# A hybrid mLSTM, attention and expert layer: shorter VectorE chains in the head norm, the gates' maximum and the convolution, with the bias copies later and the value pool opened early

## The chip, the core and the metric

One core of a Trainium2 chip runs the whole layer for 1024 tokens in one launch. The metric is the device time of that launch in microseconds, the median of several runs. The engines are TensorE (PE, with its weight loads as PEld), VectorE (DVE), ScalarE (ACT), GpSimd (POOL) and SyncE (SP), which here only issues DMAs. Each engine works through its own list of instructions in order; engines wait for one another by semaphores.

## The reference

x has 1024 tokens of 1024 channels. What is computed, cut to what matters:

```python
h = rms_norm(x, norm1_g)
u, vm, z, ipre, fpre, qa, ka, va = split(h @ w_in)          # 512 each, the gates 4 each
c = silu(causal_short_conv(u, conv_w, conv_b))              # 4 taps
hm = mlstm_chunkwise(qm, km, vm, ipre + ig_b, fpre + fg_b)  # 4 heads x 128, chunks of 128
ym = sigmoid(z) * (rms_norm(hm, mh_norm_g) + skip_m * c)
ya = combine(dilated_branch(qh, kh, vh, rel_bias, w, d) for 3 patterns)   # 8 heads x 64
x = x + concatenate([ym, ya]) @ w_out
h2 = rms_norm(x, norm2_g)
x = x + peer(h2)   # 8 heads, 128x128 product keys, top 16: 128 experts of 16384 a token
```

In `mlstm_chunkwise` each head's output is h = num / max(|den|, exp(-m)), and the norm over its 128 channels follows. The stabiliser m is a running maximum, carried from chunk to chunk as max(b_last + m, m_loc). For a token, `peer` takes gelu(h2 . u_e) times a gate for each of its experts e and sums the rows v_e.

## The kernel before

Tokens lie in eight tiles of 128, in three groups: tiles 0 and 1 (group 0), 2 to 5 (group 1), 6 and 7 (group 2). For each group come a norm and transpose of x, the products with w_in (values vm and gate z in `project_values`, gates in `project_gates`, u with the convolution in `project_conv`, attention's q, k, v in `project_attention`), attention woven with the mLSTM's chunks, w_out (`acco`), the products with w_query (`accq`) and the top-k picks. A product is done in three passes of rounded halves (high by high, low by high, high by low): ScalarE rounds a weight block (`wh`, L168), VectorE takes the remainder (`wl`, L170), and SP loads the block (`wr`, L166).

The experts are done in two ways. For group 1 all 16384 experts are computed densely on TensorE: `pu` (h2 by u) and `pv` (by v), after the gates have been spread over the experts by products `pg` and a copy to memory (`gate_d`, `gg`). For groups 0 and 2 the 128 experts of each token are gathered by indirect DMAs that GpSimd issues (L801), 128 of 512 KB for each tile and direction, in the order U0 U1 V0 V1 U6 V6 U7 V7. VectorE consumes a U gather in one instruction of 128x1024 (L813, `gt<-gt,h2s`, with a small read of the sum behind it), a V gather of tiles 6 and 7 likewise (L858), and TensorE consumes those of V0 and V1 (`pov`, L844). Gathers begin once group 0's picks are known and run beside everything that follows.

The order of each engine's instructions isn't the program's text: a scheduler of the framework keeps a modelled timeline and puts out each engine's list by it, so an edit at one place can move instructions at others. Pools set further limits: a pool that takes over another's memory waits for its last reader.

What the change and the prediction touch:

- `skew` (L132 to L134): eight copies of the position bias to memory, one per attention head, 128x1152 floats; attention's `bt` loads (L491) read them.
- `project_conv` (L255 to L278): per channel block of 128, ScalarE copies the product to `uh` behind a halo of three columns (L266 to L268), VectorE makes the first tap with the bias into `cy` (L270) and adds three more (L273), then ScalarE's sigmoid and VectorE's product follow (L275, L276).
- `project_values` (L280) with its pool "sa" and the evictions `ev`.
- `gates` (L361 to L395): softplus on ScalarE, a cumulative sum `bc` by scans (L368), `gi` (L369), then per tile a running maximum `mr` (L372) whose start is the carried maximum `mst`, and the next `mst` from its last column (L373); four rows are transposed to columns by TensorE (`pc`, L387).
- the end of each mLSTM head (L455 to L472): `sm` holds five columns for two tiles; |den| and its maximum (L457, L458), reciprocal, its square, the scaled sum of squares (L459 to L461), `rstd` (L159 on VectorE, the power at L161 on GpSimd), the product (L463), the normed head `hn` (L465), its transpose `pth` (L468).

Of the kernel before, what the change touches and what calls it, by code (L numbers as in the profile page):

```python
# [20 lines left out]
P = 128  # L21
# [22 lines left out]
def hybrid_layer(ctx, tc, x, g1, w_in, w_if, conv_w, conv_b, wq, wk, if_b, mh_g, skip, qn_g, kn_g,  # L44
# [86 lines left out]
    skew_d = {}  # L131
    for h in range(AH):  # L132
        skew_d[h] = dram.tile([P, RL], F32, name=f"skew{h}")
        nc.sync.dma_start(skew_d[h], rel_d[h:h + 1].to_broadcast([P, RL]))  # L134

# [121 lines left out]
    def project_conv(g, th, tl):  # L257
# [3 lines left out]
        with pool("su") as st:  # L261
            for blk in range(2):
                accs = by_channel(stream(w_in, blk, th, tl, n, True, "u"), n)
                for h, a in enumerate(accs, 2 * blk):
                    uh = st.tile([P, 3 + W], F32, name="uh", bufs=2)
                    nc.vector.tensor_copy(uh[:, 0:3], halo[:, h])  # L266
                    nc.scalar.copy(uh[:, 3:], a)
                    nc.vector.tensor_copy(halo[:, h], uh[:, W:W + 3])  # L268
                    y = st.tile([P, W], F32, name="cy", bufs=2)
                    nc.vector.tensor_scalar(y, uh[:, 0:W], cw_s[:, h, 0:1], cb_s[:, h:h + 1],  # L270
                                            op0=ALU.mult, op1=ALU.add)
                    for j in range(1, 4):
                        nc.vector.scalar_tensor_tensor(y, uh[:, j:j + W], cw_s[:, h, j:j + 1], y,  # L273
                                                       op0=ALU.mult, op1=ALU.add)
                    nc.scalar.activation(uh[:, 0:W], y, AF.Sigmoid)  # L275
                    nc.vector.tensor_tensor(y, y, uh[:, 0:W], op=ALU.mult)  # L276
                    c_d[g, h] = dram.tile([P, W], F32, name=f"c{g}{h}")
                    nc.sync.dma_start(c_d[g, h], y)  # L278

    def project_values(g, th, tl):  # L280

        n = GROUPS[g][1]
        W = n * P
        with pool("sa") as st:
            token_blocks(g, st, 2, vm_d, "vm", th, tl)
# [69 lines left out]
    def gates(g, cl, ml, gi, gf):  # L355
# [10 lines left out]
        for c in range(n):  # L366
            f = gf[:, c * P:(c + 1) * P]
            nc.vector.tensor_tensor_scan(bc[:, c], f, f, 0.0, op0=ALU.add, op1=ALU.bypass)  # L368
        nc.vector.tensor_tensor(gi, gi, bc, op=ALU.subtract)  # L369
        for c in range(n):  # L370
            t = tile0 + c
            nc.vector.tensor_tensor_scan(mr[:, c], gi[:, c], gi[:, c], mst[:, t:t + 1], op0=ALU.max, op1=ALU.max)  # L372
            nc.vector.tensor_tensor(mst[:, t + 1:t + 2], mr[:, c, P - 1:P], bc[:, c, P - 1:P], op=ALU.add)  # L373
        pc = pst.tile([P, 4, n, MH], F32, name="pc", tag="tp")
# [23 lines left out]
    def mlstm(g, half, h, ml, cols, mix):  # L398
# [59 lines left out]
        nc.vector.tensor_tensor(sm[:, 1], sm[:, 1], ecol[:, 1, :, h], op=ALU.max)  # L458
        nc.vector.reciprocal(sm[:, 2], sm[:, 1])  # L459
        nc.vector.tensor_tensor(sm[:, 3], sm[:, 2], sm[:, 2], op=ALU.mult)  # L460
        nc.vector.tensor_tensor(sm[:, 3], sm[:, 3], sm[:, 0], op=ALU.mult)  # L461
        r = rstd(sm[:, 3], P, HT, ml, "rm")
        nc.vector.tensor_tensor(sm[:, 4], r, sm[:, 2], op=ALU.mult)  # L463
        hn = ml.tile([P, HT, P], F32, name="hn", tag="w2m", bufs=5 if g == 0 else 6)
# [414 lines left out]
    project_conv(0, *hx)  # L879
    project_values(0, *hx)  # L880
    project_attention(0, *hx)
    mx = Scope("mx", "right")
    mix = zq.tiles.tile([P, KD, GROUPS[0][1] * P], F32, name="mix0", tag="z")
    drain(weave(attention(0, mx.tiles, mix), mlstm_half(0, 0, mx.tiles, cols, mix), 4))
    mx.close()
    hx = channels_in(1, hs.tiles)
    pt_ = Scope("pt0", "right")
    drain(queries(0, ql.tiles, "left", cl.tiles, mix))
    for t in range(2):
        pick(pt_.tiles, 0, t, cl.tiles)  # L890
    pt_.close()
    project_values(1, *hx)
    cols = project_gates(1, cm.tiles, *hx)
# [134 lines left out]
```

## Time and profile before

| | us |
|---|---|
| median of 3 runs | 3063.17 |
| lowest and highest | 3061.2, 3078.7 |
| the profiled execution | 3072.45 |
| its span in the trace | 3070.7 |
| busy: TensorE, VectorE | 2752.9, 2355.9 |
| busy: GpSimd, ScalarE | 1423.7, 1231.2 |

The span runs from the first to the last instruction of the trace; the profiled execution's own time is 1.75 us longer. The mean granted clock of TensorE over the span is 0.932 of full speed. A row of waits names the waiting engine, the line, what it waited for, and the sum, count and longest of such waits. Durations of matmuls overlap, so a mean duration is longer than the distance from one to the next.

### The profile page before, as it was taken

The numbers are of one execution on the slowest core, as the hardware profiler recorded it, in microseconds if no ns is written. First come the engines' busy times: TensorE is split into PE (matmuls) and PEld (weight loads), VectorE is DVE, ScalarE is ACT, GpSimd is POOL, SyncE is SP. The second block draws the span as 40 slices with busy tenths as digits, with TensorE's granted clock in tenths as the row PEclk, the third lists the DMA queues.
The fourth block names the chain that finished last, engine by engine and source line by source line (L and its number), as shares of the span: only waits on it lengthen the run. The fifth ranks groups of instructions, "written<-read, shape, count | busy, mean of one in ns | idle before, by whom it ended". The sixth has DMA issues, their size and how long they took to land.

```text
span 3070.7 us, 43024 instructions
## 1 busy us (share of the span) xinstructions
PE 2752.9 (90%) x14382; PEld 2174.1 (71%) x14382; DVE 2355.9 (77%) x5611; ACT 1231.2 (40%) x2271; POOL 1423.7 (46%) x1139
## 2 busy tenths in 40 slices
PE   6978757798849999889888999999999999999999
PEld 5868557576637565567655887887888787888787
DVE  4559887679874697758874888888998888898853
ACT  4643323354413323589985222332332232333222
POOL 0100567447673444544553455455555555555510
PEclk9979878587869998899998999999999999999999
DMA  6644789789898898798889999999999999999952
GB/s 196 182 149 125 263 296 338 267 317 312 311 334 294 288 322 291 235 330 297 316 298 310 321 335 319 317 335 327 335 329 356 335 315 336 338 337 317 334 181 76
DMA packets 370900, 891.52 MB, mean 290 GB/s; under 512 B 34120, under 2 KB 135496, under 8 KB 366581
## 3 DMA queue, kind: packets, MB, share of 16 engines
q0 software_dynamic: 147456, 536.94, 49.4%
q1 hardware_dynamic: 209076, 307.78, 30.6%
q10 hardware_dynamic: 14144, 44.05, 3.8%
q8 instruction: 113, 1.85, 0.2%
q14 instruction: 111, 0.90, 0.1%
HBM read 831.97 MB, written 61.38 MB: 291 GB/s over the span
## 4 chain that ended last, share of the span: by engine, by line
PE 31%; DMA 7%; issue 7%; DVE 6%; POOL 4%; ACT 2%; POOLq 0%; DVEq 0%; SPq 0%; ACTq 0%
DMA gg<-gate_d 5%; PE pu L154 5%; PE pu L153 5%; PE pu L155 5%; PE pv L154 5%; PE pv L155 5%; PE pv L153 5%; POOL gt L801 4%; DVE hot L722 1%; PE pg L737 1%; DMA gt<-in_expert_u_dram,idx 1%; ACT gs L738 1%; DMA vr<-in_expert_v_dram 1%; PE pov L844 1%; DVE gt L813 1%
## 5 line engine op out<-in xcount | busy, mean ns | idle before, releaser
L801 POOL DMA_INDIRECT gt<-in_expert_u_dram,idx x512 | 679.0, 1326 | 629.3 <-DVE gt L813 370.8
L813 DVE SCALAR_TENSOR_TENSOR gt<-gt,h2s 128x1024 f32<-128x1024 f32 x512 | 617.5, 1219 | 79.5 <-DMA gt<-in_expert_u_dram,idx 78.8
L801 POOL DMA_INDIRECT gt<-in_expert_v_dram,idx x256 | 342.2, 1337 | 281.5 <-DVE acc L858 237.3
L154 PE MATMUL pv<-vlo,dah 128*128 128x512 f32 x1024 | 402.8, 394 | 14.2 <-DVE vlo L790 14.2
L801 POOL DMA_INDIRECT gt<-in_expert_v_dram,idxt x256 | 270.1, 1055 | 310.6 <-PE pov L844 247.8
L153 PE MATMUL pu<-h2th,uhi 128*128 128x512 f32 x1024 | 406.4, 397 | 1.2 <-ACT da L763 1.2
L155 PE MATMUL pu<-h2th,ulo 128*128 128x512 f32 x1024 | 406.3, 397 | 0.7 <-DVE ulo L758 0.7
L154 PE MATMUL pu<-h2tl,uhi 128*128 128x512 f32 x1024 | 406.5, 397 | 0.0
L155 PE MATMUL pv<-vhi,dal 128*128 128x512 f32 x1024 | 401.0, 392 | 0.0
L788 ACT CAST vhi<-vr 128x512 fp32r<-128x512 f32 x256 | 158.2, 621 | 459.2 <-PE pv L155 411.8
L858 DVE SCALAR_TENSOR_TENSOR acc<-gt,act,acc 128x1024 f32<-128x1024 f32 x256 | 327.8, 1281 | 16.3 <-DMA gt<-in_expert_v_dram,idx 14.0
L153 PE MATMUL pv<-vhi,dah 128*128 128x512 f32 x1024 | 317.6, 394 | 13.9 <-ACT dah L149 11.9
L168 ACT CAST wh<-wr 128x512 fp32r<-128x512 f32 x291 | 178.6, 621 | 292.2 <-DMA wr<-in_w_in_dram 54.8
L170 DVE TENSOR_TENSOR wl<-wr,wh 128x512 fp32r<-128x512 f32 x291 | 199.4, 691 | 79.0 <-ACT wh L168 71.3
L154 PEld LDWEIGHTS pv<-vlo,dah 128*128 128x128 f32 x1024 | 193.3, 189 | 61.2 <-DVE vlo L790 19.1
L153 PEld LDWEIGHTS pv<-vhi,dah 128*128 128x128 f32 x1024 | 193.3, 189 | 59.3 <-ACT dah L149 12.3
L790 DVE TENSOR_TENSOR vlo<-vr,vhi 128x512 fp32r<-128x512 f32 x256 | 175.2, 686 | 76.5 <-ACT vhi L788 74.4
L756 ACT CAST uhi<-ur 128x1024 fp32r<-128x1024 f32 x128 | 134.5, 1051 | 235.7 <-PE pu L154 228.1
L153 PEld LDWEIGHTS pu<-h2th,uhi 128*128 128x128 f32 x1024 | 192.7, 188 | 49.8 <-issue 1.7
L154 PEld LDWEIGHTS pu<-h2tl,uhi 128*128 128x128 f32 x1024 | 192.8, 188 | 47.6 <-issue 2.5
L155 PEld LDWEIGHTS pu<-h2th,ulo 128*128 128x128 f32 x1024 | 192.8, 188 | 46.8 <-DVE ulo L758 1.3
L155 PEld LDWEIGHTS pv<-vhi,dal 128*128 128x128 f32 x1024 | 193.6, 189 | 42.1
(280 smaller groups left out, 5727.2 us busy)
## 6 DMA issues: line engine op xcount, KB each, us to landing
ur<-in_expert_ut_dram SPq DMA_DIRECT2D x128, 512.0 KB
vr<-in_expert_v_dram SPq DMA_DIRECT2D x256, 256.0 KB
wr<-in_w_in_dram SPq DMA_DIRECT2D x144, 256.0 KB
gate_d<-gs ACTq DMA_DIRECT2D x32, 1024.0 KB
gg<-gate_d SPq DMA_DIRECT2D x16, 2048.0 KB
wr<-in_w_query_dram SPq DMA_DIRECT2D x96, 256.0 KB
wr<-in_w_out_dram SPq DMA_DIRECT2D x48, 256.0 KB
gt<-in_expert_u_dram,idx POOLq DMA_INDIRECT x512
```

Source lines behind the costliest of these rows:

```text
L153: nc.tensor.matmul(ps, lh, rh, start=first, stop=False)
L154: nc.tensor.matmul(ps, lh, rl, start=False, stop=False)
L155: nc.tensor.matmul(ps, ll, rh, start=False, stop=last)
L168: nc.scalar.copy(wh, wr)
L170: nc.vector.tensor_tensor(wl, wr, wh.bitcast(F32), op=ALU.subtract)
L722: nc.vector.tensor_tensor(o, ids[:, side, None, c0:c0 + half].to_broadcast(full), key128, op=ALU.is_equal)
L756: nc.scalar.copy(uh, ur)
L788: nc.scalar.copy(vh, vr)
L790: nc.vector.tensor_tensor(vl, vr, vh.bitcast(F32), op=ALU.subtract)
L801: nc.gpsimd.indirect_dma_start(out=gt, out_offset=None, in_=table, in_offset=bass.IndirectOffsetOnAxis(ap=idx[:, j:j + 1], axis=0))
L813: nc.vector.scalar_tensor_tensor(gt, gt, 1.0, h2, op0=ALU.mult, op1=ALU.mult, accum_out=pr[:, j:j + 1])
L858: nc.vector.scalar_tensor_tensor(acc, gt, COEF[t][:, j:j + 1], acc, op0=ALU.mult, op1=ALU.add)
```

## The change

Four edits. The end of each head loses the reciprocal and two more VectorE operations: with d = max(|den|, exp(-m)), the factor on num is (sum of squares / 128 + EPS d d) to the power -0.5, formed in two combined instructions and one power on GpSimd. The carried maximum of the gates is formed by one reduction over each tile and one scan over the tiles, so that each tile's running maximum no longer hands over to the next. The convolution's first tap, with its bias, is an Identity activation on ScalarE that reads the scale and the bias as columns. The bias copies stand in the text after group 0's products, and the pool of group 1's values is opened before the pool of group 0's picks, in its own place.

```diff
@@ -129,9 +129,11 @@
         nc.sync.dma_start(rel_d, rv)
 
     skew_d = {}
-    for h in range(AH):
-        skew_d[h] = dram.tile([P, RL], F32, name=f"skew{h}")
-        nc.sync.dma_start(skew_d[h], rel_d[h:h + 1].to_broadcast([P, RL]))
+
+    def skew(heads):
+        for h in heads:
+            skew_d[h] = dram.tile([P, RL], F32, name=f"skew{h}")
+            nc.sync.dma_start(skew_d[h], rel_d[h:h + 1].to_broadcast([P, RL]))
 
 
     halo = consts.tile([P, MH, 3], F32, name="halo")
@@ -267,8 +269,7 @@
                     nc.scalar.copy(uh[:, 3:], a)
                     nc.vector.tensor_copy(halo[:, h], uh[:, W:W + 3])
                     y = st.tile([P, W], F32, name="cy", bufs=2)
-                    nc.vector.tensor_scalar(y, uh[:, 0:W], cw_s[:, h, 0:1], cb_s[:, h:h + 1],
-                                            op0=ALU.mult, op1=ALU.add)
+                    nc.scalar.activation(y, uh[:, 0:W], AF.Identity, scale=cw_s[:, h, 0:1], bias=cb_s[:, h:h + 1])
                     for j in range(1, 4):
                         nc.vector.scalar_tensor_tensor(y, uh[:, j:j + W], cw_s[:, h, j:j + 1], y,
                                                        op0=ALU.mult, op1=ALU.add)
@@ -277,11 +278,11 @@
                     c_d[g, h] = dram.tile([P, W], F32, name=f"c{g}{h}")
                     nc.sync.dma_start(c_d[g, h], y)
 
-    def project_values(g, th, tl):
+    def project_values(g, th, tl, st=None):
 
         n = GROUPS[g][1]
         W = n * P
-        with pool("sa") as st:
+        with (nullcontext(st) if st else pool("sa")) as st:
             token_blocks(g, st, 2, vm_d, "vm", th, tl)
             for blk in range(2):
                 accs = by_channel(stream(w_in, 4 + blk, th, tl, n, True, "z"), n)
@@ -367,10 +368,14 @@
             f = gf[:, c * P:(c + 1) * P]
             nc.vector.tensor_tensor_scan(bc[:, c], f, f, 0.0, op0=ALU.add, op1=ALU.bypass)
         nc.vector.tensor_tensor(gi, gi, bc, op=ALU.subtract)
+
+        top = ml.tile([MH, n], F32, name="top")
+        nc.vector.tensor_reduce(top, gi, AX.X, ALU.max)
+        nc.vector.tensor_tensor_scan(mst[:, tile0 + 1:tile0 + n + 1], top, bc[:, :, P - 1],
+                                     mst[:, tile0:tile0 + 1], op0=ALU.max, op1=ALU.add)
         for c in range(n):
             t = tile0 + c
             nc.vector.tensor_tensor_scan(mr[:, c], gi[:, c], gi[:, c], mst[:, t:t + 1], op0=ALU.max, op1=ALU.max)
-            nc.vector.tensor_tensor(mst[:, t + 1:t + 2], mr[:, c, P - 1:P], bc[:, c, P - 1:P], op=ALU.add)
         pc = pst.tile([P, 4, n, MH], F32, name="pc", tag="tp")
         for q in range(4):
             row = gi
@@ -456,11 +461,10 @@
         dn = num[:, :, P]
         nc.vector.scalar_tensor_tensor(sm[:, 1], dn, -1.0, dn, op0=ALU.mult, op1=ALU.max)
         nc.vector.tensor_tensor(sm[:, 1], sm[:, 1], ecol[:, 1, :, h], op=ALU.max)
-        nc.vector.reciprocal(sm[:, 2], sm[:, 1])
-        nc.vector.tensor_tensor(sm[:, 3], sm[:, 2], sm[:, 2], op=ALU.mult)
-        nc.vector.tensor_tensor(sm[:, 3], sm[:, 3], sm[:, 0], op=ALU.mult)
-        r = rstd(sm[:, 3], P, HT, ml, "rm")
-        nc.vector.tensor_tensor(sm[:, 4], r, sm[:, 2], op=ALU.mult)
+
+        nc.vector.scalar_tensor_tensor(sm[:, 2], sm[:, 1], EPS, sm[:, 1], op0=ALU.mult, op1=ALU.mult)
+        nc.vector.scalar_tensor_tensor(sm[:, 3], sm[:, 0], 1.0 / P, sm[:, 2], op0=ALU.mult, op1=ALU.add)
+        nc.gpsimd.tensor_tensor(sm[:, 4], sm[:, 3], mhalf.to_broadcast([P, HT]), op=ALU.pow)
         hn = ml.tile([P, HT, P], F32, name="hn", tag="w2m", bufs=5 if g == 0 else 6)
         nc.vector.tensor_tensor(hn, num[:, :, 0:P], sm[:, 4, :, None].to_broadcast([P, HT, P]), op=ALU.mult)
         pt = pml.tile([P, HW], F32, name="pth", tag="ml")
@@ -878,18 +882,21 @@
     cols = project_gates(0, cm.tiles, *hx)
     project_conv(0, *hx)
     project_values(0, *hx)
+    skew(range(AH))
     project_attention(0, *hx)
     mx = Scope("mx", "right")
     mix = zq.tiles.tile([P, KD, GROUPS[0][1] * P], F32, name="mix0", tag="z")
     drain(weave(attention(0, mx.tiles, mix), mlstm_half(0, 0, mx.tiles, cols, mix), 4))
     mx.close()
     hx = channels_in(1, hs.tiles)
+    sv = Scope("sv", "right")
     pt_ = Scope("pt0", "right")
     drain(queries(0, ql.tiles, "left", cl.tiles, mix))
     for t in range(2):
         pick(pt_.tiles, 0, t, cl.tiles)
     pt_.close()
-    project_values(1, *hx)
+    project_values(1, *hx, sv.tiles)
+    sv.close()
     cols = project_gates(1, cm.tiles, *hx)
     project_conv(1, *hx)
     project_attention(1, *hx)
```

What becomes of the lists: in SP's list one weight block stands between the first skew copy and the other seven, where all eight stood ahead of it; the blocks after it and the `bt` loads keep their places. In VectorE's list 235 gather consumers stand ahead of the last `hn` of group 1, 246 before. In TensorE's list 39 rows of `acco` move from behind the last `pth` of group 1 to ahead of it, 36 rows of `pov` from ahead of the first `pg` to behind it, and 52 of `pu` from ahead of the last `pg` to behind it; 99 rows of `pu` stand between the last `pg` and the first `pv`, 71 before, and the last 24 rows of V1's `pov` stand behind the first `pv`.

VectorE's list at the last head but one of group 1, before (`L813` are gather consumers, `pr_s` their sums, `rmo` GpSimd's power):

```order
L457 SCALAR_TENSOR_TENSOR sm<-num 128x2
L813 SCALAR_TENSOR_TENSOR gt,pr_s<-gt,h2s 128x1024
L458 TENSOR_TENSOR sm<-sm,ecol 128x2
L459 RECIPROCAL sm<-sm 128x2
L813 SCALAR_TENSOR_TENSOR gt,pr_s<-gt,h2s 128x1024
L460 TENSOR_TENSOR sm<-sm 128x2
L461 TENSOR_TENSOR sm<-sm 128x2
L813 SCALAR_TENSOR_TENSOR gt,pr_s<-gt,h2s 128x1024
L159 TENSOR_SCALAR rm<-sm 128x2
L813 SCALAR_TENSOR_TENSOR gt,pr_s<-gt,h2s 128x1024 x2
L463 TENSOR_TENSOR sm<-rmo,sm 128x2
L465 TENSOR_TENSOR hn<-num,sm 128x256
```

and now (`L817` are the gather consumers, `ya` is a part of attention's result):

```order
L462 SCALAR_TENSOR_TENSOR sm<-num 128x2
L463 TENSOR_TENSOR sm<-sm,ecol 128x2
L817 SCALAR_TENSOR_TENSOR gt,pr_s<-gt,h2s 128x1024
L465 SCALAR_TENSOR_TENSOR sm<-sm 128x2
L542 TENSOR_TENSOR ya<-po,den 128x2x4x64
L466 SCALAR_TENSOR_TENSOR sm<-sm 128x2
L817 SCALAR_TENSOR_TENSOR gt,pr_s<-gt,h2s 128x1024
L469 TENSOR_TENSOR hn<-num,sm 128x256
```

Of the five gather consumers between the first `sm` and `hn` two are left, with one operation of attention in between.

TensorE's list where group 1's gate products end, before (`pif` are the gates, `accu` the convolution's input; 46 rows of `accu` follow, then `pc`):

```order
L155 MATMUL pif<-hth,wl 64x512
L153 MATMUL pif<-hth,wh 64x512
L154 MATMUL pif<-htl,wh 64x512
L155 MATMUL pif<-hth,wl 64x512
L192 MATMUL accu<-hth,wh 128x512
L192 MATMUL accu<-htl,wh 128x512
L192 MATMUL accu<-hth,wl 128x512
```

and now:

```order
L157 MATMUL pif<-hth,wl 64x512
L155 MATMUL pif<-hth,wh 64x512
L156 MATMUL pif<-htl,wh 64x512
L157 MATMUL pif<-hth,wl 64x512
L392 MATMUL pc<-ident,gi 128x4 x4
L392 MATMUL pc<-ident,row 128x4 x12
L194 MATMUL accu<-hth,wh 128x512
L194 MATMUL accu<-htl,wh 128x512
L194 MATMUL accu<-hth,wl 128x512
```

`pc` stands right behind `pif`; 44 rows of `accu` stand ahead of `pif`.

## Rows read from the trace of the kernel before

**Rows 1.** Page: busy us (share) xinstructions, and tenths by slice.

```profile
PE 2752.9 (90%) x14382; PEld 2174.1 (71%) x14382; DVE 2355.9 (77%) x5611; ACT 1231.2 (40%) x2271; POOL 1423.7 (46%) x1139
...
PE   6978757798849999889888999999999999999999
...
DVE  4559887679874697758874888888998888898853
```

**Rows 2.** Busy us by stretch: PE, PEld, DVE, ACT, POOL; clock, DMA share, GB/s.

```profile
352.00:412.00 60.00, 34.31 (x139) 25.51 (x139) 53.37 (x104) 17.33 (x26) 43.88 (x30) 0.78 0.88 304
826.00:930.00 104.00, 58.68 (x303) 48.38 (x302) 78.56 (x179) 26.18 (x63) 68.08 (x53) 0.67 0.91 325
930.00:1300.00 370.00, 350.84 (x2032) 218.86 (x2030) 263.37 (x1326) 129.12 (x261) 164.88 (x160) 0.94 0.84 285
1300.00:1560.00 260.00, 218.81 (x1670) 172.93 (x1669) 203.06 (x768) 241.78 (x489) 133.07 (x125) 0.98 0.87 311
1690.00:3070.00 1380.00, 1358.94 (x5861) 1101.34 (x5859) 1120.85 (x1498) 403.91 (x607) 667.03 (x502) 1.00 0.88 308
```

**Rows 3.** TensorE's waits, 1300 to 1560 us: total us, times, longest.

```profile
PE pg L737 <- ACT gs L738: 11.5, 15, 3.1
```

**Rows 4.** TensorE's waits, 826 to 930 us.

```profile
PE pth L468 <- DVE hn L465: 33.8, 2, 19.3
```

**Rows 5.** VectorE in time order: start, duration, instruction, idle before.

```profile
867.57 0.15 DVE L457 SCALAR_TENSOR_TENSOR sm<-num 128x2 f32<-128x2 f32 x1
868.98 1.23 DVE L813 SCALAR_TENSOR_TENSOR gt<-gt,h2s 128x1024 f32<-128x1024 f32 x1 [1.25 <-DMA gt<-in_expert_u_dram,idx]
...
874.68 0.16 DVE L159 TENSOR_SCALAR rm<-sm 128x2 f32<-128x2 f32 x1
...
878.08 0.42 DVE L465 TENSOR_TENSOR hn<-num,sm 128x256 f32<-128x256 f32 x1
```

**Rows 6.** VectorE's groups by line, 326 to 905 us.

```profile
L813 DVE SCALAR_TENSOR_TENSOR gt<-gt,h2s 128x1024 f32<-128x1024 f32 x246 | 297.7, 1218 | 50.6 <-DMA gt<-in_expert_u_dram,idx 50.2
...
L813 DVE DVE_READ_ACCUMULATOR gt<-gt,h2s 128x1 f32 x246 | 19.7, 80 | 0.0
```

**Rows 7.** TensorE's waits, 222 to 352 us.

```profile
PE accvm L192 <- ACT ev L304: 8.3, 1, 8.3
```

**Rows 8.** TensorE's waits, 352 to 412 us.

```profile
PE pc L387 <- DVE row L380: 12.0, 1, 12.0
...
PE pc L387 <- DVE gi L369: 3.0, 1, 3.0
```

**Rows 9.** SP's queue in time order, 18 to 25 us.

```profile
18.65 5.33 SPq L134 DMA_DIRECT2D skew<-rel_d  x8
24.09 0.61 SPq L166 DMA_DIRECT2D wr<-in_w_in_dram  x1
```

**Rows 10.** ScalarE in time order, at 39 us.

```profile
39.14 0.62 ACT L168 CAST wh<-wr 128x512 fp32r<-128x512 f32 x1 [6.56 <-DMA wr<-in_w_in_dram]
```

**Rows 11.** Tile sm, one of its operations: ns min/median/max.

```profile
L461 DVE TENSOR_TENSOR sm<-sm x16: 144/158/190, 87.3 to 1266.6; 128x2 f32<-128x2 f32 x16
```

**Rows 12.** Line L270 over the whole run.

```profile
L270 DVE TENSOR_SCALAR cy<-uh,cw_s,cb_s x12: 393/408/547, 50.3 to 735.9; 128x256 f32<-128x256 f32 x8, 128x512 f32<-128x512 f32 x4
```

**Rows 13.** Groups by line, 352 to 412 us.

```profile
L192 PE MATMUL accu<-hth,wh 128*128 128x512 f32 x32 | 13.9, 434 | 0.0
...
L250 ACT ACTIVATE gi<-pif,ifb_s 4x512 f32<-4x512 f32 x1 | 0.7, 677 | 0.0
...
L369 DVE TENSOR_TENSOR gi<-gi,bc 4x512 f32<-4x512 f32 x1 | 0.7, 674 | 0.0
...
L373 DVE TENSOR_TENSOR mst<-mr,bc 4x1 f32<-4x1 f32 x4 | 0.6, 144 | 0.0
```

**Rows 14.** TensorE's groups by line, 930 to 1300 us.

```profile
L844 PE MATMUL pov<-gt,wv 128*32 128x512 f32 x608 | 85.6, 636 | 14.4 <-DMA gt<-in_expert_v_dram,idxt 13.7 <-issue 0.5
```

**Rows 15.** TensorE's waits, 1640 to 1690 us.

```profile
PE pv L153 <- ACT dah L149: 11.9, 1, 11.9
```

More of the change, by code (lines that the diff above doesn't have):

```diff
@@ L1 @@
 import math
-from contextlib import ExitStack
+from contextlib import ExitStack, nullcontext
 from itertools import chain
```

## The prediction

> **What bounds the kernel now.** I read the page first, then busy times by stretch, then TensorE's waits in the stretches where it sits idle, and last, instruction by instruction, what VectorE did while TensorE waited. The page shows TensorE busy for 2752.9 us of 3070.7, and in the last two slices TensorE stands at nine tenths while VectorE falls to five and three [rows 1]: the end is TensorE's. The change removes no matmul. So the end moves only as far as TensorE's idle time (317.8 us) moves, and the question is where that idle time lies.
>
> The stretches tell [rows 2]. From 1690 us on TensorE is busy 1358.9 of 1380: nothing to win there. From 930 to 1300 it is busy 350.8 of 370, so there it is the bound again. Before that it isn't: 34.3 of 60 (352 to 412 us), 58.7 of 104 (826 to 930), with VectorE at 53.4 of 60 and 78.6 of 104 and the DMA engines at 0.88 to 0.91. From 1300 to 1560 ScalarE is busy 241.8 of 260, and TensorE waits there for ScalarE's gate products, 11.5 us in all [rows 3].
>
> The longest waits of the early part are two, 33.8 us together, of the transpose pth for the normed head hn [rows 4]. In the chain before the first of them five gather consumers of 1.22 us, most of them waiting for their gather, stand among the small operations on VectorE [rows 5]: the first operation (L457) starts at 867.57, hn at 878.08. That is 10.5 us for eight instructions of 0.15 to 0.42 us. VectorE works in order, and 246 such consumers fill 297.7 us of the 579 us from 326 to 905, with 50.2 us of waiting for gathers before them [rows 6]. So up to the last head of group 1 (the four middle token tiles) VectorE's queue sets the pace, and what stands ahead of a head in that queue counts, more than the few operations of its chain. Two shorter waits belong to the other edits: 8.3 us of the value product accvm for its eviction [rows 7], and 12.0 and 3.0 us of pc for the gates' rows [rows 8].
>
> **The change part by part.**
>
> Bias copies. SP issues eight skew copies (128x1152 floats, 576 KB each) from 18.65 to 24.0 us and the next weight block only at 24.09 [rows 9]; ScalarE waits 6.56 us for a weight at 39.14 [rows 10]. In the new order one weight block comes ahead of seven of the copies; the remaining blocks still follow. The bounds are 0 and -6.6; I take -4, since the next block is still behind the copies. The skews' first readers (bt) keep their places behind them on SP.
>
> Head chain. Eight VectorE operations and one power on GpSimd become five and one: three fewer in each of 16 heads. A removed one takes about 0.158 us [rows 11], so twelve heads up to the end of group 1 give 36 x 0.158 = 5.7 us, group 2 another 1.9 where TensorE is the bound.
>
> First convolution tap. VectorE loses twelve instructions [rows 12]: eight of 256 columns, four in each of groups 0 and 2, at the median of 0.408 us, 1.6 us a group, and four of 512 columns in group 1 at up to 0.547, 2.2 us; 3.8 us up to the end of group 1. ScalarE gets them: the gates' Identity with a bias column took 0.68 us for 512 columns [rows 13]. Bounds for a tap of 512: 0.55 (as VectorE) and 1.4 (twice that row); I take 0.7. ScalarE is busy 17.3 of 60 us in that stretch [rows 2], which hides it. The new wait, for VectorE's copy of the halo, holds up the weight roundings behind it on ScalarE; TensorE waits for these. Where the cover is gone this costs the longer tap, 12 x 0.15 = 1.8 us at 0.7, 12 x 0.85 = 10 us at 1.4; I take 0.
>
> [...]
>
> Gates' maximum. In group 1 four single-column additions of 0.144 us go; a reduction over a 4x512 tile (0.674 us by the subtraction gi of that size) and one short scan (0.144, as an addition) come [rows 13]: VectorE's work is even, within 0.3 us. What goes is the back and forth in which each tile's maximum waits for the one before. But in the new order 12 gather consumers stand between the forget gate's copy and the last row, where there were 11 (five weight remainders less): the chain is filled again. I take 0.
>
> Value pool and the convolution. With its pool open early the second values' evictions need not wait for the top-k pool: the 8.3 us go [rows 7], bound 0. The same order puts the first 44 matmuls of the convolution ahead of the 24 gate matmuls, where 46 stood behind them as cover for the gates' chain. A matmul of that stretch takes 34.31 / 139 = 0.247 us [rows 2] (the 0.434 of one [rows 13] overlaps its neighbours), so 44 make 10.9 us by which the chain starts later on TensorE, and pc, right behind the gates now, waits uncovered. VectorE has its gathers to do meanwhile, 16 instead of 14 ahead of the gates, so of the 10.9 us only what VectorE itself sits idle counts. I set that against the 8.3: zero together, bounds -8 and +11.
>
> Order of the gathers. The scheduler moves more than the edits: 235 gather consumers instead of 246 stand ahead of the last head of group 1. 11 x (1.22 + 0.08) = 14.3 us [rows 5, 6]. With 5.7 and 3.8 that makes 23.8; other work that came ahead (39 rows of the output projection acco and their remainders, adds of the mixing) takes back 6.0, counted over all VectorE rows ahead of that head at the durations of their kinds. Net -17.8.
>
> What follows that head. It comes 4 + 17.8 = 21.8 us earlier, and 39 acco rows are done by then, at the stretch's mean 350.84 / 2032 = 0.173 us [rows 2] 6.7 us of matmul: TensorE's idle time is 28.5 us less. Behind it the 11 postponed gathers come ahead of V0's. The matmuls pov that read V0 and V1 (0.141 us each: 85.6 / 608 [rows 14]) waited 13.7 us for them [rows 14]; bounds 0 and +14 (11 consumers of 1.3 us); I take +3, because 36 rows of pov also move behind the gate products. In the stretch that ScalarE bounds TensorE then has less to fill with: 52 pu matmuls fewer ahead of the last gate product, 52 x 0.232 (1358.94 / 5861 [rows 2]) = 12.1 us. A third of that shortens the stretch, the rest is idle: +8, bounds 0 and +12. Last, pv's first wait of 11.9 us [rows 15] gets 28 more pu matmuls of cover, 6.5 us: -6, bounds 0 and -11.9.
>
> Sum: -28.5 + 3 + 8 - 6 = -23.5 us. Against the profiled execution, 3072.45, that is 3049; the median of the runs shown, 3063.2, is 9 us below it, and the same difference from the median gives 3039.7, forecast 3040.
>
> **The rivals.**
>
> All waits go and stay gone. If pth's 33.8, accvm's 8.3 and the start's 6.6 vanish in full and nothing comes in their place, 48.7 us go: about 3015. For it: TensorE is 95% busy right behind, so a gain there carries. Against it: VectorE and the DMA engines are nearly full in the same stretch.
>
> The change doesn't do what it says. The chains get shorter in instructions, but each small operation still stands behind a gather consumer; if the gathers' arrival (DMA 0.88 to 0.91 [rows 2]) sets the pace, the 11 postponed ones are only paid later, in w_out and V0. Then the start's 4 us remain: about 3060.
>
> Slower: the gates' chain uncovered. From the gate matmuls to the last row TensorE has nothing, and VectorE reaches the forget gate's copy before ScalarE has it. It decides once ScalarE hands over the forget gate more than some 8 us after VectorE is ready for it, for then the value pool's gain is spent. Price: the 10.9 us; the 11 late gathers then push V1's, for which 24 rows of its pov, now behind the first pv, would hold TensorE up by 11 x 1.3 = 14 us more. +25 with none of the gains is about 3088. For it speaks that pc waited 15 us even with its cover [rows 8]; against it, that VectorE had work in 53.4 of those 60 us.
>
> **How the numbers follow.** The forecast 0.5 (own range 3022 to 3056, from the bounds of its terms), all waits gone 0.2, nothing gained 0.2, slower 0.1. A measurement of this kernel tells about 1%, 30.6 us, from no change: faster is below 3032.5, slower above 3093.8. Faster: 0.2 and three tenths of the forecast's 0.5, 0.35. Slower by that much: four tenths of the last rival and a little for unknown prices, 0.07. The rest, 0.58, is the same. The range goes down to 3005, past the case of all waits gone, and up to 3080.
>
> **What would show it.** Right: the last pth of group 1 about 22 us earlier and its waits under 15 us; accvm's 8.3 gone; pc's wait above 15 us; the taps on ScalarE near 0.7 us; TensorE's idle time about 294 us, with more of it from 1300 to 1560. Wrong: a last pth at the old time (the gathers' arrival paced it), the same pth earlier but the first pu not (absorbed behind it), or pu and pv matmuls waiting on the late pov.

## The result and the profile after

The changed kernel takes 3037.0 us (median of 6 runs, 3032.0 to 3054.1); the kernel before takes 3072.4 (6 runs: the three of the section on the time before and three more). The ratio is 0.9896, with a 95% interval of 0.9866 to 0.9926: faster by 1.0%. The forecast was 3040, in a range of 3005 to 3080. The profiled span fell from 3070.7 to 3033.4 us.

The page after, parts 1 and 2, as in [rows 1]:

```profile
PE 2735.0 (90%) x14382; PEld 2149.5 (71%) x14382; DVE 2353.3 (78%) x5553; ACT 1234.4 (41%) x2279; POOL 1400.0 (46%) x1139
...
PE   6978657788869999888889999999999999999999
...
DVE  4559887579975897668873798888898888889863
```

TensorE is still the last, VectorE still falls off in the last two slices. But its busy time, 2752.9 us before, is 17.9 us less, with the same 14382 matmuls. The stretches, with the limits of [rows 2]:

```profile
352.00:412.00 60.00, 23.73 (x91) 16.81 (x90) 53.27 (x101) 14.93 (x21) 45.30 (x33) 0.67 0.86 294
826.00:930.00 104.00, 78.20 (x477) 63.90 (x476) 81.69 (x182) 33.20 (x87) 58.39 (x49) 0.82 0.93 333
930.00:1300.00 370.00, 347.22 (x2010) 215.25 (x2013) 269.06 (x1320) 152.59 (x304) 170.02 (x164) 0.93 0.84 289
1300.00:1560.00 260.00, 219.97 (x1620) 171.48 (x1612) 211.86 (x772) 238.34 (x466) 134.22 (x123) 0.97 0.87 305
1690.00:3033.00 1343.00, 1321.58 (x5696) 1070.29 (x5695) 1101.57 (x1468) 393.29 (x590) 661.58 (x501) 1.00 0.89 313
```

From 826 to 930 us TensorE is busy 78.2 us instead of 58.7, and its granted clock is 0.82 instead of 0.67; from 352 to 412 it is busy less, 23.7 against 34.3. The waits of [rows 4], [rows 7] and [rows 8] are read again, in the stretches that answer to theirs. First come those of the heads, 805 to 900 us:

```profile
PE pth L472 <- DVE hn L469: 17.8, 3, 12.7
```

Then come those of the gates, 352 to 412 us:

```profile
PE pc L392 <- DVE gi L370: 15.5, 1, 15.5
PE pc L392 <- DVE row L385: 7.9, 1, 7.9
...
PE pc L392 <- DVE row L390: 3.1, 1, 3.1
```

The transposes of the heads wait 17.8 us instead of 33.8. The gates' pc waits 26.5 us, where it waited 15.0 in [rows 8] and 1.2 more for its last row: the convolution's matmuls that had covered it now stand ahead of the gates. accvm's 8.3 us are gone, and so are the 11.9 us of the first pv [rows 15]. The last head of group 1 on VectorE (start, duration, instruction, idle before):

```profile
865.60 0.16 DVE L462 SCALAR_TENSOR_TENSOR sm<-num 128x2 f32<-128x2 f32 x1
866.54 1.23 DVE L817 SCALAR_TENSOR_TENSOR gt<-gt,h2s 128x1024 f32<-128x1024 f32 x1 [0.78 <-DMA gt<-in_expert_u_dram,idx]
...
867.69 0.16 DVE L463 TENSOR_TENSOR sm<-sm,ecol 128x2 f32<-128x2 f32 x1
...
869.36 0.16 DVE L465 SCALAR_TENSOR_TENSOR sm<-sm 128x2 f32<-128x2 f32 x1
...
870.62 0.16 DVE L466 SCALAR_TENSOR_TENSOR sm<-sm 128x2 f32<-128x2 f32 x1
...
873.85 0.42 DVE L469 TENSOR_TENSOR hn<-num,sm 128x256 f32<-128x256 f32 x1 [0.61 <-POOL sm L467]
```

The first of its operations starts at 865.60, hn at 873.85: 8.25 us to the last of five operations, since gather consumers still stand between them. The same head in the kernel before, first and last of eight operations:

```profile
893.97 0.15 DVE L457 SCALAR_TENSOR_TENSOR sm<-num 128x2 f32<-128x2 f32 x1
...
905.01 0.42 DVE L465 TENSOR_TENSOR hn<-num,sm 128x256 f32<-128x256 f32 x1
```

That is 11.0 us, so the chain itself gave 2.8 us here. The larger part is that it begins 28.4 us earlier. The last pth starts at 874.3 us, before at 905.5. VectorE's gather consumers up to there, as in [rows 6]:

```profile
L817 DVE SCALAR_TENSOR_TENSOR gt<-gt,h2s 128x1024 f32<-128x1024 f32 x235 | 284.7, 1218 | 49.6 <-DMA gt<-in_expert_u_dram,idx 49.0
...
L817 DVE DVE_READ_ACCUMULATOR gt<-gt,h2s 128x1 f32 x235 | 18.7, 80 | 0.0
```

With their reads they take 303.4 us, 14.0 less than the 317.4 of before. The wait for their gathers stays as it was, 49.0 us against 50.2.

The start, SP's queue and ScalarE, as in [rows 9] and [rows 10]:

```profile
19.05 0.57 SPq L136 DMA_DIRECT2D skew<-rel_d  x1
19.71 0.54 SPq L168 DMA_DIRECT2D wr<-in_w_in_dram  x1
20.30 4.50 SPq L136 DMA_DIRECT2D skew<-rel_d  x7
```

```profile
41.26 1.93 ACT L170 CAST wh<-wr 128x512 fp32r<-128x512 f32 x3 [4.95 <-DMA wr<-in_w_in_dram]
```

One block went ahead of seven copies, and ScalarE waits 4.95 us for the next one, until 41.26; before it went on at 39.14. Nothing is gained there. The tap on ScalarE (ns min/median/max):

```profile
L272 ACT ACTIVATE cy<-uh,cb_s,cw_s x12: 589/602/817, 52.5 to 730.4; 128x256 f32<-128x256 f32 x8, 128x512 f32<-128x512 f32 x4
```

It takes 0.60 us for 256 columns and 0.82 for 512, where VectorE took 0.41 and at most 0.55 [rows 12].

### The profile page after: what moved, and what is told of

Read it like the earlier page. It is cut to its first block, busy times and chain, and to the rows that moved or that the text cites. A ratio compares the mean times of both kernels' runs of the same rounds, so it can differ in the third digit from the quotient of the medians.

```text
span 3033.4 us, 42961 instructions
## 1 busy us (share of the span) xinstructions
PE 2735.0 (90%) x14382; PEld 2149.5 (71%) x14382; DVE 2353.3 (78%) x5553; ACT 1234.4 (41%) x2279; POOL 1400.0 (46%) x1139
## 4 chain that ended last, share of the span: by engine, by line
PE 31%; DMA 7%; DVE 6%; issue 6%; POOL 4%; ACT 2%; POOLq 0%; DVEq 0%; ACTq 0%
DMA gg<-gate_d 5%; PE pu L157 5%; PE pu L156 5%; PE pu L155 5%; PE pv L156 5%; PE pv L157 5%; PE pv L155 5%; POOL gt L805 4%; DMA gt<-in_expert_u_dram,idx 1%; DVE hot L726 1%; PE pg L741 1%; DVE gt L817 1%; PE pov L848 1%; PE accq L194 1%; DMA vr<-in_expert_v_dram 1%
## 5 line engine op out<-in xcount | busy, mean ns | idle before, releaser
L805 POOL DMA_INDIRECT gt<-in_expert_u_dram,idx x512 | 662.9, 1295 | 622.9 <-DVE gt L817 379.5
L817 DVE SCALAR_TENSOR_TENSOR gt<-gt,h2s 128x1024 f32<-128x1024 f32 x512 | 618.8, 1220 | 80.5 <-DMA gt<-in_expert_u_dram,idx 79.4
L156 PE MATMUL pv<-vlo,dah 128*128 128x512 f32 x1024 | 402.1, 393 | 11.9 <-DVE vlo L794 11.9
```

The source lines that it names most:

```text
L156: nc.tensor.matmul(ps, lh, rl, start=False, stop=False)
L805: nc.gpsimd.indirect_dma_start(out=gt, out_offset=None, in_=table, in_offset=bass.IndirectOffsetOnAxis(ap=idx[:, j:j + 1], axis=0))
L817: nc.vector.scalar_tensor_tensor(gt, gt, 1.0, h2, op0=ALU.mult, op1=ALU.mult, accum_out=pr[:, j:j + 1])
```

## The experiments

Three theories went into the runs. A: what counts is how many gather consumers stand in VectorE's list ahead of the last head of group 1. B: each edit is worth the instructions that it removes, wherever the order puts the rest. C: the end moves with TensorE's granted clock and not with that count. Each edit was run alone (only_), and all but the bias copies were also left out of the full change (no_); the value pool and the bias copies, one edit in the section on the change, count as two here, which makes five. Two kernels (hold) leave every edit out and move only the consumers. Each kernel's trace is one execution. Ratios are to the kernel before, run beside each; all 95% intervals are in the table at the end of this section.

**The head chain alone.** Of the diff, only this part is taken:

```diff
-        nc.vector.reciprocal(sm[:, 2], sm[:, 1])
-        nc.vector.tensor_tensor(sm[:, 3], sm[:, 2], sm[:, 2], op=ALU.mult)
-        nc.vector.tensor_tensor(sm[:, 3], sm[:, 3], sm[:, 0], op=ALU.mult)
-        r = rstd(sm[:, 3], P, HT, ml, "rm")
-        nc.vector.tensor_tensor(sm[:, 4], r, sm[:, 2], op=ALU.mult)
+        nc.vector.scalar_tensor_tensor(sm[:, 2], sm[:, 1], EPS, sm[:, 1], op0=ALU.mult, op1=ALU.mult)
+        nc.vector.scalar_tensor_tensor(sm[:, 3], sm[:, 0], 1.0 / P, sm[:, 2], op0=ALU.mult, op1=ALU.add)
+        nc.gpsimd.tensor_tensor(sm[:, 4], sm[:, 3], mhalf.to_broadcast([P, HT]), op=ALU.pow)
```

> The kernel before with the shorter head chain alone. In its new order 226 gather consumers stand ahead of the last head of group 1 (246 before, 235 in the full change). Theory A, VectorE's queue ahead of that head: 20 consumers (26 us) and 36 small operations (5.7 us) less, about a third of it taken back by other work that comes ahead: the last pth 20 us earlier or more and the time 15 to 25 us below before. Theory B, each edit is worth its own instructions wherever the order puts the rest: 5.7 to 8 us below before. Theory C, the end moves with TensorE's granted clock only: no relation to the count; TensorE's busy time falls as much as the span.

Measured: 3010.4 us, ratio 0.9771 (0.9730 to 0.9811). That is 67 us below before, where theory A allowed 25 at most, and 1.3% below the full change, whose interval it does not touch. Theory B falls at once: 36 operations of 0.16 us don't make 67 us. Theory C as it was put falls too: TensorE's busy time fell by 22.7 us (2752.9 to 2730.2), the span by 59.1.

**The tap alone.**

```diff
-                    nc.vector.tensor_scalar(y, uh[:, 0:W], cw_s[:, h, 0:1], cb_s[:, h:h + 1],
-                                            op0=ALU.mult, op1=ALU.add)
+                    nc.scalar.activation(y, uh[:, 0:W], AF.Identity, scale=cw_s[:, h, 0:1], bias=cb_s[:, h:h + 1])
```

> The kernel before with the first convolution tap on ScalarE alone. 230 gather consumers ahead of the last head of group 1 (246 before). Theory A: 16 consumers (21 us) and 3.8 us of taps less, a part taken back by other work: 12 to 20 us below before. Theory B: 0 to 5 us below before. [...]

Measured: 3032.7, ratio 0.9841 (0.9800 to 0.9882), though each tap is longer on ScalarE than on VectorE (0.60 us at the median, up to 0.82; in the kernel before 0.41, at most 0.55). It leaves the heads' own operations as they were, and yet their last pth comes 38.6 us earlier. The taps that VectorE no longer does up to there are 3.8 us of that, so the edit works mainly through the order, with 16 consumers fewer ahead.

**The head chain left out** (the full change with the first diff undone).

> The full change with the old head chain (eight VectorE operations and the power). 246 gather consumers ahead of the last head of group 1 again, as before. Theory A: nearly the whole gain is lost, within 8 us of before, 25 to 30 us above the full change; the waits of pth for hn back to about 34 us. Theory B: 5.7 to 8 us above the full change.

Measured: 3068.1, ratio 0.9972 (0.9943 to 1.0001). With 246 consumers ahead again the gain of the other four edits is gone, and TensorE's waits for hn, 860 to 905 us, are nearly what they were before (33.8):

```profile
PE pth L473 <- DVE hn L470: 29.8, 2, 17.7
```

**The value pool left out** (project_values opens its own pool again).

> The full change without the early value pool. 224 gather consumers ahead of the last head of group 1 (235 in the full change), accvm's wait of about 8 us for its eviction back, the convolution behind the gate products as before. Theory A: 11 consumers (14 us) less against the 8 us: 0 to 8 us below the full change. Theory B: 8 us above the full change.

Measured: 3027.4, ratio 0.9825 (0.9782 to 0.9867). It is below the full change, which is theory A's direction and not theory B's; the two intervals just touch.

**The consumers moved and nothing else.** The chains are those of before. The last head of group 1 writes a zero that a gather consumer of U1 needs, so the consumers from there on have to stand behind that head:

```diff
+    flag = consts.tile([P, 1], F32, name="flag")
...
+        if g == 1 and half == 1 and h == MH - 1:
+            nc.vector.tensor_scalar(flag, hn[:, 0, 0:1], 0.0, None, op0=ALU.mult)
         pt = pml.tile([P, HW], F32, name="pth", tag="ml")
...
         for j in range(P):
+            if t == 1 and j == 98:
+                nc.vector.tensor_tensor(h2[:, 0:1], h2[:, 0:1], flag, op=ALU.add)
```

> The kernel before, every chain as it was, with one thing more: the last head of group 1 writes a zero that U1's 98th gather consumer adds to its operand, so that no more than 226 gather consumers can stand ahead of that head (246 before; 226 is the count of the head chain alone). Two small VectorE instructions are added, nothing is removed. Theory A, the number of gather consumers ahead of the head sets its time, 2.4 us each (the first six kernels: 905.0 us at 246, 847.2 at 224): the last hn at 850 to 865 us, the time 40 to 60 us below before. Theory B, the shorter chains themselves gave the gain: the last hn at about 900 and the time within 5 us of before.

Measured: 3063.5, ratio 0.9961 (0.9935 to 0.9987). Theory A holds for the head, at a lower price than expected, and fails for the time. The last pth comes earlier with no chain shortened, by 23.3 us and not by the 40 to 55 expected. That is 1.2 us for each of the 20 consumers, about what one keeps VectorE busy with its read (1.22 + 0.08). VectorE's busy time up to that pth fell by as much, from 683.1 to 660.4 us. But the time follows by less than half: of the 23.3 us, 4.7 are left at the end of the trace, and the medians differ by 11. TensorE's idle time fell by 15 us up to that head and rose by 30 behind it. Its waits from the first pv on, of this kernel:

```profile
PE pv L154 <- ACT vhi L791: 34.6, 12, 15.2
PE pv L155 <- DVE vlo L793: 12.1, 6, 5.1
```

and of the kernel before:

```profile
PE pv L154 <- DVE vlo L790: 14.2, 8, 4.8
PE pv L153 <- ACT dah L149: 11.9, 1, 11.9
PE pv L153 <- ACT vhi L788: 2.0, 3, 0.8
```

That is 46.7 us against 28.1. Why these waits grew was not tried apart.

The same kernel with 72 in place of 98, which leaves 200 consumers ahead:

> As the one with 226, but 200 consumers ahead of the last head of group 1. Theory A without a limit: the last hn at about 795 us. Theory A with what follows counted: the last hn no earlier than attention's and the projections' work lets it, about 820 to 840, and the postponed gathers put 96 rows of pov behind the first pv, so the time is no better than with 226 and may be 0 to 20 us worse. Theory B: as before, 3072 us.

Measured: 3049.8, ratio 0.9911 (0.9878 to 0.9944), the last pth at 862.4 us. That is 0.9 us for each of 46 consumers, and the head comes no earlier than with 226 in the head chain alone (860.3), nor as early as the 820 to 840 that the expectation allowed. VectorE's busy time up to there fell by 50 us (683 to 633), but it idles 229 us instead of 222; what it waits for in place of the work is not shown. The time is a little better than when held at 226, not worse as expected, though the two intervals overlap.

**The gates' maximum alone** (the diff's part in `gates`).

> The kernel before with the gates' maximum alone. 251 gather consumers ahead of the last head of group 1 (246 before). Theory A: the last hn 5 to 12 us later, the time 0 to 12 us above before. Theory B: 0 to 3 us below before.

Measured: 3069.8, ratio 0.9978 (0.9950 to 1.0005): no difference that the runs can tell, with the last pth 17 us later.

**The value pool alone** (`sv` and the argument of `project_values`).

> The kernel before with the early value pool alone. 250 gather consumers ahead of the last head of group 1 (246 before), accvm's wait of 8.3 us gone, the convolution's first 44 matmuls ahead of the gate matmuls. Theory A: 10 us later by the consumers, 0 to 8 us back by the wait: 0 to 10 us above before. Theory B: 8 us below before.

Measured: 3043.4, ratio 0.9893 (0.9855 to 0.9930). Both theories miss: the last pth is 7 us later than before, with 30 us of waits for hn, and the kernel is as fast as the full change. (Its trace is one of its longer executions, 3053.0.) The stretches up to the last pth and from there to the first pg show where the time goes, for this kernel and for the one before:

```profile
0.00:912.50 912.50, 695.57 (x4075) 581.73 (x4075) 688.18 (x1872) 359.71 (x750) 370.65 (x299) 0.82 0.76 257
913.00:1271.00 358.00, 339.65 (x2074) 212.95 (x2073) 261.29 (x1324) 131.35 (x270) 164.13 (x162) 0.99 0.88 302
```

```profile
0.00:905.50 905.50, 688.98 (x4075) 580.46 (x4075) 683.10 (x1863) 363.68 (x753) 387.99 (x295) 0.82 0.76 256
905.50:1297.00 391.50, 369.14 (x2140) 234.68 (x2141) 278.98 (x1358) 136.08 (x276) 177.96 (x171) 0.93 0.84 287
```

From the last head to the first pg it takes 358 us instead of 391.5. TensorE's idle time there is 18 and 22 us, so nearly all of it is busy time, 29.5 us less: some 70 matmuls (nearly all of acco and pov) have moved behind the first pg, by estimate some 12 us at the 0.17 of that stretch (369.14 / 2140), and the others run at a granted clock of 0.99 instead of 0.93, worth by an estimate from these two clocks 369 x (1 - 0.93 / 0.99) = 22 us at most.

**The bias copies alone.**

> The kernel before with the later bias copies alone: SP issues one weight block ahead of seven of the eight copies, the lists of the other engines stay as they were but for one weight remainder. Prediction's step: 4 us below before. Theory A (the order of the consumers): within 4 us of before, since 246 stay ahead of the last head; ScalarE still waits 5 us or more for the next block behind the copies.

Measured: 3075.5, ratio 0.9991 (0.9958 to 1.0024). The edit alone gives nothing. It also tells how far two traces of one order can differ: TensorE's list is that of before up to the last pth, VectorE is as busy up to there (683.5 us against 683.1), and yet that pth comes 12.5 us later, at a granted clock of 0.81 instead of 0.82. So the 7 and 17 us of the pool and the gates alone are not clear of chance.

**The tap left out, the gates left out, the head chain with the pool.**

> The full change with the first tap back on VectorE. 230 consumers ahead of the last head of group 1 (235 in the full change). Theory A by the line through the first six kernels (2.4 us for a consumer, 3069 at 246): 12 us below the full change, about 3030. Theory B: 4 to 6 us above the full change, about 3042. [...]

> The full change with the old gates' maximum. 225 consumers ahead of the last head of group 1 (235 in the full change, 224 without the pool). Theory A by the same line: 24 us below the full change, about 3018. Theory B: 0 to 3 us above it, about 3039.

> The head chain and the early pool together, alone. 232 consumers ahead of the last head of group 1 (226 with the head chain alone, 250 with the pool alone). Theory A by the line: about 3035, 25 us slower than the head chain alone. If the two gains measured alone add (67 and 31 us below before): about 2980. If the pool's gain was the place of the late work and not its wait: near the head chain alone, 3010.

Measured: 3042.0, ratio 0.9899 (0.9867 to 0.9932); 3028.7, 0.9858 (0.9820 to 0.9896); 3032.2, 0.9863 (0.9824 to 0.9901). The third hits theory A's line (3035) and shows that gains measured alone don't add: the head chain loses 22 us when the pool joins it. The second is 8 us below the full change, where 24 were expected, and their intervals overlap; the first is level with it, where 12 below were expected.

The table has all kernels by the number of consumers ahead of the last head. All run the same 4076 TensorE instructions, if not in one order, up to that head's pth. The columns give its start, VectorE's busy time, TensorE's idle time and the granted clock up to there:

| kernel | consumers | pth, us | VectorE busy, us | TensorE idle, us | clock | ratio | interval |
| --- | --- | --- | --- | --- | --- | --- | --- |
| gates alone | 251 | 923 | 689 | 216 | 0.81 | 0.9978 | 0.9950 to 1.0005 |
| pool alone | 250 | 913 | 688 | 217 | 0.82 | 0.9893 | 0.9855 to 0.9930 |
| before | 246 | 906 | 683 | 217 | 0.82 | 1 | |
| bias copies alone | 246 | 918 | 684 | 216 | 0.81 | 0.9991 | 0.9958 to 1.0024 |
| without the head chain | 246 | 901 | 679 | 212 | 0.82 | 0.9972 | 0.9943 to 1.0001 |
| full change | 235 | 874 | 663 | 206 | 0.85 | 0.9896 | 0.9866 to 0.9926 |
| head chain and pool | 232 | 856 | 661 | 185 | 0.85 | 0.9863 | 0.9824 to 0.9901 |
| tap alone | 230 | 867 | 659 | 193 | 0.85 | 0.9841 | 0.9800 to 0.9882 |
| without the tap | 230 | 868 | 660 | 189 | 0.85 | 0.9899 | 0.9867 to 0.9932 |
| head chain alone | 226 | 860 | 654 | 186 | 0.85 | 0.9771 | 0.9730 to 0.9811 |
| without the gates | 225 | 844 | 650 | 189 | 0.87 | 0.9858 | 0.9820 to 0.9896 |
| without the pool | 224 | 848 | 649 | 180 | 0.86 | 0.9825 | 0.9782 to 0.9867 |
| before, held at 226 | 226 | 882 | 660 | 201 | 0.84 | 0.9961 | 0.9935 to 0.9987 |
| before, held at 200 | 200 | 862 | 633 | 177 | 0.84 | 0.9911 | 0.9878 to 0.9944 |

Leaving out the two held kernels, the pth follows the count closely: a line through the twelve has 2.7 us for one consumer and a correlation of 0.97. The ratio follows it less well, with 0.83. But 2.7 us is not what one consumer costs, since these kernels differ in more than the count. Where the count alone was moved, one cost 1.2 and 0.9 us. The rest of the line is time in which VectorE idles ahead of the head (pth less busy time): 221 to 235 us in the five kernels with 246 and more consumers, 194 to 211 in the seven with fewer, 222 and 229 in the held ones. Why it falls with the edits and not with the count was not tried apart.

## Why the prediction was right, and which of its steps were not

The time came out 3 us from the forecast, and the reason that it gave, VectorE's list ahead of group 1's heads, is the one that the runs bear out for the heads: the order decides, and edits that leave the heads alone move them all the same. That the number was hit is luck, though. The sum behind it is in good part wrong, with errors that cancel: the change is worth 35 us in the medians (3072.4 to 3037.0) and 37.3 in the profiled spans, not 23.5; the time was hit so closely because the kernel before also measured 9 us longer over all six of its runs than over the first three. The prediction put faster, by its own 1%, below 3032.5 us and thought the same likelier (0.58); 3037.0 lies just on that side, though 35 us under the kernel before as measured beside it.

**"The change removes no matmul. So the end moves only as far as TensorE's idle time (317.8 us) moves."** This step failed. Of the profiled 37.3 us, 17.9 are busy time. Here are the stretch up to the last pth of the full change and those further on (before's stand above):

```profile
0.00:874.30 874.30, 668.60 (x4074) 558.28 (x4074) 663.37 (x1794) 366.42 (x762) 354.26 (x284) 0.85 0.77 259
874.30:1251.00 376.70, 354.82 (x2034) 226.55 (x2035) 283.02 (x1353) 134.84 (x273) 173.24 (x164) 0.92 0.84 289
1635.00:3026.00 1391.00, 1376.32 (x5952) 1109.74 (x5950) 1133.64 (x1518) 408.46 (x614) 683.66 (x519) 1.00 0.90 313
```

The same 4076 instructions took 669 us instead of 689, at a clock of 0.85 instead of 0.82. In all fourteen kernels busy time times clock (to two digits) up to that point lies between 564 and 578 us, over clocks from 0.81 to 0.87. The ends of the range of clocks are the gates alone and the gates left out:

```profile
0.00:922.50 922.50, 706.60 (x4074) 590.08 (x4074) 689.49 (x1869) 363.04 (x754) 378.72 (x300) 0.81 0.75 254
```

```profile
0.00:845.00 845.00, 655.59 (x4076) 551.60 (x4076) 650.72 (x1775) 365.90 (x763) 348.11 (x275) 0.87 0.77 262
```

Of the 31.2 us by which the last pth came earlier, 11 are idle time and 20 are faster matmuls. That fewer gaps raised the clock is not shown: the bias copies alone have before's idle time there (216 us, 217 before) and a lower clock (0.81, 0.82 before).

**"39 acco rows are done by then."** This was misread. The same TensorE instructions stand up to that pth in both kernels; the 39 rows went from ahead of the first pg to behind it. The sentence on acco in the section on the change is wrong in this too. So the term of -28.5 us of idle time was -11 (217 to 206): its 6.7 us for acco were not there, and most of the earlier head came as busy time.

**"11 x (1.22 + 0.08) = 14.3 us."** This term was right. The 11 consumers fewer make 14.0 us less of VectorE's time (317.4 to 303.4), and the other work up to that pth brings VectorE's busy time down by 19.7 in all (683.1 to 663.4), where the prediction had 17.8 net. What it left out is VectorE's idle time, for which it had no term: 222.4 us up to that pth before, 210.9 now, 11.5 less. With it the pth comes 31.2 us earlier, for 21.8 forecast. It is not the wait for the U gathers, which stayed at 49.0 us (50.2 before); it is about what the two traces of one order, before and the bias copies alone, differ by (12). Its cause stays open.

**The start, -4.** It gave nothing: the next block still waits behind seven copies (ScalarE for 4.95 us, until 41.26), and the edit alone measures 0.9991.

**The tap, hidden on ScalarE.** Hidden it was, but for 2.7 us in all that VectorE waited for it, in four waits. It is longer than taken, too: 0.60 us for 256 columns and 0.82 for 512, where 0.7 was taken for 512. The edit alone made the kernel 1.6% faster, and inside the full change it makes no difference (0.9899 without it).

**Value pool and gates, zero together.** This was right as a sum: accvm's 8.3 us went, pc's wait grew by 10.3, and the attention products accqk start at 413 us as they did at 412. The rival of the uncovered gates has its wait, but not its price.

**V0 and V1 (+3), the gate products (+8), the first pv (-6).** From the last pth to the first pg TensorE's idle time is 22 us in both; from there to the first pv it rose by 5 (44 to 49); from there to TensorE's last matmul, the wait ahead of the first pv included, it fell by 13 (28 to 15). With -11 that is -19 us of idle time, for -23.5 forecast: near in the sum, and not in its terms (+3, +8 and -6 behind the head, where 0, +5 and -13 were measured). The signs that the prediction named for being right came in part: pth earlier by 31 us and not 22, its waits at 17.8 and not under 15, pc's wait above 15, TensorE's idle time at 298.4 and not 294.

**The rival "all waits gone"**, 3015, is nearly what the head chain alone gave, 3010, but not by its mechanism: the waits for hn are still 15.7 us there. **"The change doesn't do what it says"**, 3060, is out for the whole; of the five edits alone, two gave nothing that the runs can tell, the bias copies and the gates' maximum.

What stays open: why the stretch behind the last head runs at a clock of 0.99 with the pool alone and 0.97 with the head chain alone, and at 0.93 before and 0.92 in the full change and when held at 226:

```profile
0.00:860.30 860.30, 674.78 (x4074) 565.92 (x4074) 653.69 (x1785) 358.84 (x752) 345.26 (x275) 0.85 0.76 257
860.30:1218.00 357.70, 337.95 (x2025) 220.97 (x2025) 286.44 (x1350) 134.47 (x274) 171.05 (x162) 0.97 0.88 303
```

```profile
0.00:882.20 882.20, 680.71 (x4075) 573.51 (x4075) 660.37 (x1823) 364.04 (x753) 356.07 (x276) 0.84 0.75 253
882.00:1267.00 385.00, 354.77 (x2061) 228.60 (x2062) 299.38 (x1389) 135.89 (x274) 178.09 (x169) 0.92 0.85 289
```

The idle time there goes with it only loosely: 18 us with the pool alone, 20 with the head chain alone, 30 when held at 226, but 22 both before and in the full change. Whether it is the cause was not tried apart. So the count tells of the head and not of the end, and the clock remains a part of what moves the end.

The fastest version is the kernel before with the head chain alone, 3010 us, ahead of both kernels; why the other four edits take back half of its gain is not shown beyond the 9 consumers that they bring ahead of the head.

## What to carry to other kernels

Where a scheduler orders an engine's list, an edit's worth isn't in its instructions: count what its order puts ahead of the work that others wait for. Price it by moving the order and nothing else: a line through kernels that differ in several things gave 2.7 us for a consumer, the moved order 1.2, near the 1.22 us that one takes on VectorE with the 0.08 of its read. And follow the work past the point where it comes earlier, for here 23 us won at the head left 5 at the end of the trace and 11 in the medians. Measure each part of a bundle alone, too: one of five parts beats the whole, and two are worth nothing that could be measured. Last, read TensorE's granted clock beside its busy time: here half of the gain, 17.9 of 37.3 us, came as busy time, with no matmul removed.

## What was not expected of the hardware

Run to run, one kernel's time moves with the mean granted clock: over the runs of the kernel before beside the experiments, 3058 to 3100 us, the clock lay between 0.921 and 0.937, and by and large the longer runs had the lower one (0.935 and 0.934 in the two shortest, 0.926 and 0.923 in the two longest). Between kernels it is much the same: the head chain alone, the fastest, ran at 0.944 to 0.951.

Read in stretches of 2 us, the clock of the kernel before up to its last head (0 to 904 us) is 1.00 in 266 of 452 stretches, 0.50 in 129, in between in the other 57 and never lower. In the full change (0 to 874 us) it is 1.00 in 285 of 437, 0.50 in 109, in between in 43. By and large the kernels with less of TensorE's idle time up to the head have the higher clock there: the five with 212 to 217 us have 0.81 or 0.82, the nine with 177 to 206 have 0.84 to 0.87. Within the nine it is not so, with 0.84 at 177 us and 0.85 at 206, and what moves the clock was not shown.
